# Weight rows of the first down-projection pass sent for during the last weight pair

## The chip, the cores and the metric

The kernel runs on one core of a Trainium2 chip. The metric is the device time of one execution in microseconds (us), taken as the median of the runs; lower is better. The profile and the trace come from one further execution, recorded by the hardware profiler.

The engines are PE (matrix products; PEld is its weight load), DVE (VectorE), ACT (ScalarE), POOL (GpSimd) and SP, which here only sends for transfers. POOL sends for some transfers too.

## The reference

A decoder layer: a mixing sub-layer of three branches, then a feed-forward network with a causal convolution. The change touches the second alone:

```python
h = rms_norm(x, norm_ffn_pre[l])
u = causal_dwconv(h @ w_ffn_up[l], conv_w[l], conv_b[l])
u_gate, u_val = jnp.split(u, 2, axis=-1)
f = (jax.nn.gelu(u_gate, approximate=True) * u_val) @ w_ffn_down[l]
x = x + rms_norm(f, norm_ffn_post[l])
```

There are 1024 tokens, a model width of 1024 and a hidden width of 2816, which is 22 blocks of 128 channels. Everything is float32.

## The kernel before

A product of two float32 matrices is made of three matmuls. Each operand is split into a rounded high part, made by a cast on ACT, and a low part, the difference, made by a subtraction on DVE or POOL. Function `mm3` (lines 168 to 170) issues high by high, high by low and low by high. Activations and results lie with channels in the 128 partitions and tokens along the row.

**The up-projection** runs over pairs of weight blocks, one gate block and one value block for each of the 22 hidden blocks. Pairs 5 to 21 go through `up_pairs`: each forms its 2 by 2 block product by seven products instead of eight (a Strassen scheme), each of four `mm3`. `Pair.load` sends for the weights of a pair (tiles a11, a21, a22, a12), two transfers of 128 KB for each tile, by SP into places of the pool `wp`. The places come in two classes, `self.c = i % 2`: even pairs use `whi0`, `wlo0` and `wraw0`, odd pairs `whi1`, `wlo1` and `wraw1`, with four, four and three places each (the pairs use two of the three `wraw` places at a time). Pair 21 is the last, of class 1, so that the places of class 0 are not used again once pair 20's weights have been split. `sum0` to `sum6` take the seven products out of PSUM, and `sum6` multiplies gate and value and stores the hidden block in the DRAM array `d_f`. `sum4` of the last pair calls `down_loads`, which sends for the first three rows of the down-projection.

**The down-projection** is a second such scheme, over halves of tokens, of output channels and of hidden blocks. It is seven passes (`down_pass`), each over 11 steps. A step takes an activation row f (128 hidden channels by 512 tokens, 256 KB) and a weight row u (the same 128 hidden channels by 512 output channels, 256 KB), splits both, and issues 12 matmuls into four PSUM banks named psd. Splitting is done by `step` (casts at line 1405, subtractions at line 1409): there are four places for the split u and four for the split f, so a cast for step n waits until PE has done step n - 4. The sources differ by pass:

- Pass 1: activations X, loaded from `d_f` by `f_rows` (line 1352); weights by `w_raw` (line 1363), tile name fw, 128 partitions by four runs of 512 B, into the tag `st`, which has three places. Row k + 3 can be sent for once both halves of row k's split have been made.
- Pass 2: activations R, the second half of the hidden blocks; weights Q, the sum of two blocks of the weight matrix. `Q.load` (SP) brings the first in pieces of 1 MB, 1 MB and three of 256 KB, and `Q.add` (POOL) lets an accumulating transfer add the second to it (line 1345 for both). Pieces of Q are sent for during pass 1.
- Pass 3: activations R minus another set of rows, fraw, for which there are four places; weights again by `w_raw`, into the same three places as in pass 1.

X, R and fraw rows come from `d_f`, which the pairs have written; the fraw places are those of the pairs' split weights.

**What sets the order.** Each engine works through its own queue in a fixed order, and a transfer whose place or source is not ready holds up all that SP or POOL would send after it. The order of the queues comes from a scheduler that places instructions when their operands and places are expected to be ready. `later(i, x)` tells it to put i behind x in the order, without a wait on the chip. In pass 1 both rows of step k are tied in this way to the last matmul of step k - 3.

Of the kernel before, what the change touches and what calls it, by code (L numbers as in the profile page):

```python
# [9 lines left out]
F32 = mybir.dt.float32  # L10
# [7 lines left out]
P = 128  # L18
# [10 lines left out]
NF = 22  # L29
HK = NF // 2  # L30
# [14 lines left out]
def trunk_kernel(ctx: ExitStack, tc: tile.TileContext, xT, memT, pvec, w_in, w_kv, w_upd, w_upg,  # L45
                 w_pool, w_ppool, w_pmem, w_prwkv, w_o, w_fup, w_fdn, out):
    nc = tc.nc
    V, A, G, PE, SP = nc.vector, nc.scalar, nc.gpsimd, nc.tensor, nc.sync

    const = ctx.enter_context(tc.tile_pool(name="const", bufs=1))  # L50
    wp = ctx.enter_context(tc.tile_pool(name="wp", bufs=1))
# [92 lines left out]
    def load_w(ap, nk, kp=2, c=None):  # L144
        if c is None:
            cls[0] ^= 1
            c = cls[0]
        ps = Ws()
        ps.c = c
        for k0 in range(0, nk, kp):  # L150
            load_more(ps, ap, k0, min(kp, nk - k0), kp)
        return ps
# [12 lines left out]
    def mm3(ps, w, x, start, stop):  # L165
        wh, wl = w
        xh, xl = x
        first = PE.matmul(ps, wh, xh, start=start, stop=False)  # L168
        PE.matmul(ps, wh, xl, start=False, stop=False)  # L169
        last_mm[0] = PE.matmul(ps, wl, xh, start=False, stop=stop).ins  # L170
        return first
# [36 lines left out]
    def later(i, ins, plain=False):  # L208

        tc.add_manual_dep(i if plain else i.ins, ins.name, nosync, reason="order")  # L210
# [13 lines left out]
    for k in range(KC):  # L224
        tag = ("X01", "X11", "HV", "HV")[k // 2]
# [802 lines left out]
    class Pair:  # L1028
# [46 lines left out]
            getattr(self, f"sum{n}")(ps)  # L1075

        def sum0(self, ps):
            z = [ow1.tile([P, T], F32, name=f"z{e}", tag=f"q{4 + 2 * e + self.c}") for e in range(2)]
            self.z = z
            self.c11, self.c12, self.c21, self.c22 = z[0][:, :512], z[0][:, 512:], z[1][:, :512], z[1][:, 512:]  # L1080
            self.u2 = ow.tile([P, 512], F32, name="u2", tag="xt", bufs=2)
            A.copy(self.c11, ps)
# [11 lines left out]
        def sum4(self, ps):  # L1094
            self.p7 = ps
            third = V.tensor_tensor(self.c21, self.u2, ps, op=ALU.add).ins
            if self.i == NF - 1:
                down.extend(down_loads())
                down.append(third)

        def sum5(self, ps):
# [154 lines left out]
    ahead = [load_w(w_fup[3], KC), load_w(w_fup[NF + 3], KC)]  # L1256
# [4 lines left out]
    for n in range(4):  # L1261
        j = (3, NF + 3, 4, NF + 4)[n]
# [59 lines left out]
    def panel_slots(name, tag, n0):  # L1322
        t = hf.tile([P, KC, 512], F32, name=name, tag=tag)
        return [t[:, k] for k in range(KC)] + tail_slots(name, n0)
# [26 lines left out]
    def f_rows(dst, k, n, behind=None):  # L1351
        i = SP.dma_start(dst, d_f[k][:, n * 512:n * 512 + 512])  # L1352
        if behind is not None:
            later(i, behind)
        return dst
# [5 lines left out]
    def w_raw(k, e, h, behind=None):  # L1361
        t = wp.tile([P, 512], F32, name="fw", tag="st", bufs=3).rearrange("p (j c) -> p j c", c=P)
        i = SP.dma_start(t, w_fdn[4 * e:4 * e + 4, :, HK * h + k].rearrange("j p c -> p j c"))
        if behind is not None:
            later(i, behind)
        return t

    def down_loads():

        X = panel_slots("X", "h2h0", 0)  # L1370
        return X, [(f_rows(X[k], k, 0), w_raw(k, 0, 0)) for k in range(3)]
# [22 lines left out]
    def step(x, w, places=None, behind=None):  # L1394

        n = nstep[0]
        if places is None:
            nstep[0] += 1
            f = at.tile([P, 2, 512], FR, name="f", tag=f"m{4 + n % 4}")
            u = at.tile([P, 2, 4, P], FR, name="u", tag=f"m{n % 4}")  # L1400
            u, f = ([t[:, e] for e in range(2)] for t in (u, f))
        else:
            u, f = [x.rearrange("p (j c) -> p j c", c=P) for x in places[:2]], places[2:]
        for t, src in ((u, w), (f, x)):
            hi = A.copy(t[0], src)  # L1405
            if behind is not None:
                later(hi, behind)
            on_pool = n == 1 or t is u and 3 < npass[0] < 7 and n % 2
            low = (G if on_pool else V).tensor_tensor(t[1], src, t[0].bitcast(F32), op=ALU.subtract)  # L1409
            if n < 8:  # L1410
                later(low, third if n == 0 else last_low[0] if n == 1 else last_sum[0])
        return [(u[0][:, a], u[1][:, a]) for a in range(4)], f

    log = []

    def down_pass(x, w, n, evac, side={}, post=None):
        pool, tag = ((psc, "c"), (psk, "k"))[npass[0] % 2]
        npass[0] += 1
        banks = [p_.tile([P, 512], F32, name="psd", tag=t_)
                 for p_, t_ in ((pool, tag), (psg, "g0"), (psg, "g1"), (pss, "s"))]  # L1420
        for k in range(n):
            if k in side:
                side[k]()

            if left and (n < HK or k % 2):
                for i in left.pop(0)():
                    later(i, last_mm[0])
            ws, f = step(x(k), w(k), behind=log[-3] if len(log) > 2 else None)
            if post:
                later(post(k), last_mm[0])  # L1430
            for a in range(4):
                mm3(banks[a], ws[a], f, k == 0, k == n - 1)
            log.append(last_mm[0])
        left.extend(partial(evac, a, banks[a]) for a in range(4))
# [14 lines left out]
    X, ahead, third = down  # L1449
# [6 lines left out]
    def x0(k):  # L1456
        return ahead[k][0] if k < 3 else f_rows(X[k], k, 0, log[k - 3])

    down_pass(x0, lambda k: ahead[k][1] if k < 3 else w_raw(k, 0, 0, log[k - 3]), HK, evac1,
              {3: lambda: Q.load(1, 0, 0), 5: lambda: Q.add(1, 1, 0), 7: lambda: Q.load(1, 0, 1),  # L1460
               9: lambda: Q.add(1, 1, 1)})

# [70 lines left out]
    down_pass(lambda k: X[k], lambda k: Q[k], LAST, lambda a, ps: plus(c12[a], ps), side)  # L1533
    SP.dma_start(xt, d_x1[:, :, 768:].rearrange("k p t -> p k t"))
    rest = [step(X[LAST + k], Q[LAST + k], places[k], log[k + 2 - LAST]) for k in range(HK - LAST)]
    out0(2)
    for u in left:
# [108 lines left out]
def build(arrays):  # L1646
    import numpy as np
    import concourse.bacc as bacc

    nc = bacc.Bacc("TRN2", target_bir_lowering=False, num_devices=1)  # L1650
    aps = {n: nc.dram_tensor(f"in_{n}", a.shape, mybir.dt.from_np(a.dtype), kind="ExternalInput").ap()
           for n, a in arrays.items()}
    out = nc.dram_tensor("out_T", (D, T), F32, kind="ExternalOutput").ap()
    with tile.TileContext(nc) as tc:
        trunk_kernel(tc, **aps, out=out)
    return nc
# [10 lines left out]
```

## Time and profile before

| | |
|---|---|
| median of 3 runs | 2056.73 us (2052.93 to 2056.75) |
| the profiled execution's own time | 2058.67 us |
| its span, first to last instruction | 2056.8 us |
| mean granted TensorE clock | 0.995 of full speed |
| share of busy time | PE 97%, PEld 76%, DVE 67%, ACT 52%, POOL 39% |
| SP's transfers (queue q1) | 204.44 MB, 30.7% of the 16 DMA engines' span |
| POOL's transfers (queue q0) | 14.16 MB, 4.2% |
| last matmul of the pairs, first of the down-projection | 1823.67 us, 1823.90 us |
| first and last psd matmul | 1823.90 us, 2030.69 us |

Times in the rows count from the first instruction of the span. A row of the timeline has the start, the duration, the engine, the line, the operation, the output and inputs by name, the shape and the count, and in brackets how long the engine had stood idle and what ended that. SPq is SP's queue of transfers: its rows show the sending, not the transfer. A row of transfers has the count, the size of one, and the time from sending to landing in us. In a table of stretches each engine has its busy time and, in brackets, its instructions; then come the granted clock (1.00 is full speed), the mean busy share of the 16 DMA engines, and GB/s.

### The profile page before, as it was taken

The numbers are of one execution on the slowest core, as the hardware profiler recorded it, in microseconds if no ns is written. First come the engines' busy times: TensorE is split into PE (matmuls) and PEld (weight loads), VectorE is DVE, ScalarE is ACT, GpSimd is POOL, SyncE is SP. The second block draws the span as 40 slices with busy tenths as digits, with TensorE's granted clock in tenths as the row PEclk, the third lists the DMA queues.
The fourth block names the chain that finished last, engine by engine and source line by source line (L and its number), as shares of the span: only waits on it lengthen the run. The fifth ranks groups of instructions, "written<-read, shape, count | busy, mean of one in ns | idle before, by whom it ended". The sixth has DMA issues, their size and how long they took to land. (4 is left out here: it accounts for less than half of the span.)

```text
span 2056.8 us, 34070 instructions
## 1 busy us (share of the span) xinstructions
PE 2000.2 (97%) x12246; PEld 1558.2 (76%) x12246; DVE 1378.4 (67%) x2204; ACT 1073.6 (52%) x2249; POOL 804.4 (39%) x883
## 2 busy tenths in 40 slices
PE   8999999999999999999999999999999999999997
PEld 5777767786778667776778887877678888877886
DVE  6567537663568357734596552768889888867798
ACT  7575338723773358434567343545544554444544
POOL 4521213121222121111122355655579888832441
PEclk9999999999999999999999999999999999999999
DMA  4412112120212121212525543645332222169776
GB/s 152 136 42 75 66 36 86 58 93 22 88 62 83 36 90 40 90 63 89 193 92 189 157 136 106 191 129 164 97 95 87 85 80 82 67 198 260 166 183 150
DMA packets 176714, 221.84 MB, mean 108 GB/s; under 512 B 16544, under 2 KB 128288, under 8 KB 176544
## 3 DMA queue, kind: packets, MB, share of 16 engines
q1 hardware_dynamic: 163616, 204.44, 30.7%
q0 software_dynamic: 11856, 14.16, 4.2%
q8 instruction: 97, 1.59, 0.3%
q10 hardware_dynamic: 1072, 1.05, 0.2%
q14 instruction: 73, 0.60, 0.1%
HBM read 170.30 MB, written 49.28 MB: 107 GB/s over the span
## 5 line engine op out<-in xcount | busy, mean ns | idle before, releaser
L132 POOL TENSOR_TENSOR wlo<-wraw,whi 128x256 fp32r<-128x256 f32 x472 | 412.7, 884 | 940.7 <-ACT whi L129 774.5
L168 PE MATMUL psg<-hh,whi 128*128 128x512 f32 x928 | 380.1, 410 | 2.6 <-DVE kv L315 2.6
L170 PE MATMUL psg<-hh,wlo 128*128 128x512 f32 x928 | 376.3, 406 | 0.4
L169 PE MATMUL psg<-hl,whi 128*128 128x512 f32 x928 | 375.5, 405 | 0.0
L129 ACT CAST whi<-wraw 128x256 fp32r<-128x256 f32 x472 | 182.5, 403 | 227.6 <-PE psg L169 105.7
L168 PEld LDWEIGHTS psg<-hh,whi 128*128 128x128 f32 x928 | 174.6, 188 | 43.1 <-DVE kv L315 3.8
L170 PEld LDWEIGHTS psg<-hh,wlo 128*128 128x128 f32 x928 | 174.2, 188 | 43.2 <-POOL wlo L132 5.9
L169 PEld LDWEIGHTS psg<-hl,whi 128*128 128x128 f32 x928 | 174.6, 188 | 39.4 <-issue 3.6
L1011 POOL TENSOR_TENSOR wt<-a,wt 128x256 fp32r<-128x256 f32 x136 | 156.7, 1176 | 35.6 <-ACT wt L1010 35.6
L168 PE MATMUL psd<-f,u 128*128 128x512 f32 x292 | 114.7, 393 | 3.1 <-ACT u L1405 2.4
L169 PE MATMUL psd<-f,u 128*128 128x512 f32 x292 | 114.6, 393 | 0.6 <-DVE f L1409 0.6
L170 PE MATMUL psd<-f,u 128*128 128x512 f32 x292 | 114.1, 392 | 0.0
L170 PE MATMUL psf<-h2h,wt 128*128 128x512 f32 x272 | 105.9, 389 | 1.0 <-POOL wt L1011 1.0
L169 PE MATMUL psf<-h2l,wt 128*128 128x512 f32 x272 | 105.8, 389 | 0.0
L168 PE MATMUL psf<-h2h,wt 128*128 128x512 f32 x272 | 105.8, 389 | 0.0
L1025 DVE SCALAR_TENSOR_TENSOR d<-z,pv,d 128x1023 f32<-128x1023 f32 x68 | 101.1, 1491 | 2.2
L1011 POOL TENSOR_TENSOR wt<-s,wt 128x256 fp32r<-128x256 f32 x68 | 80.3, 1201 | 3.4 <-ACT wt L1010 2.1
L686 DVE TENSOR_TENSOR HV<-ph,Hd 64x128 f32<-64x128 f32 x112 | 32.4, 289 | 72.2 <-PE ph L640 48.1
L168 PE MATMUL psf<-t,wt 128*128 128x512 f32 x204 | 79.4, 389 | 0.0
L169 PE MATMUL psf<-t,wt 128*128 128x512 f32 x204 | 79.4, 389 | 0.0
L170 PE MATMUL psf<-t,wt 128*128 128x512 f32 x204 | 79.4, 389 | 0.0
L1023 ACT ACTIVATE d<-z,pv 128x1024 f32<-128x1024 f32 x34 | 42.4, 1246 | 67.6 <-DVE z L1102 51.9
(425 smaller groups left out, 4747.0 us busy)
## 6 DMA issues: line engine op xcount, KB each, us to landing
wraw<-in_w_in SPq DMA_DIRECT2D x240, 128.0 KB, 2.4
a<-in_w_fup SPq DMA_DIRECT2D x128, 128.0 KB, 2.4
d_zg<-st SPq DMA_DIRECT2D x48, 256.0 KB, 2.7
wraw<-in_w_fup SPq DMA_DIRECT2D x80, 128.0 KB, 2.5
fw<-in_w_fdn SPq DMA_DIRECT2D x33, 256.0 KB, 4.3
fraw<-d_f SPq DMA_DIRECT2D x33, 256.0 KB, 4.5
wraw<-in_w_prwkv SPq DMA_DIRECT2D x64, 128.0 KB, 2.4
wraw<-in_w_o SPq DMA_DIRECT2D x64, 128.0 KB, 2.5
```

Of the source, the lines that this page charges most:

```text
L129: last_whi[0] = A.copy(hi, src).ins
L132: (V if lo_on_dve[0] else G).tensor_tensor(lo, src, hi.bitcast(F32), op=ALU.subtract)
L168: first = PE.matmul(ps, wh, xh, start=start, stop=False)
L169: PE.matmul(ps, wh, xl, start=False, stop=False)
L170: last_mm[0] = PE.matmul(ps, wl, xh, start=False, stop=stop).ins
L686: ready = V.tensor_tensor(HV[q, :, c + 1, e], ph[q], Hd[q], op=ALU.add).ins
L1011: low = eng.tensor_tensor(w[1][:, us], src[u], w[0][:, us].bitcast(F32), op=ALU.subtract)
L1023: A.activation(d, z, AF.Identity, scale=col("cw2", j), bias=col("cb", j))
L1025: V.scalar_tensor_tensor(d[:, n:], z[:, :T - n], col(cw, j), d[:, n:], op0=ALU.mult, op1=ALU.add)
```

## The change

Eight of the eleven weight rows of pass 1, rows 3 to 10, no longer go through `w_raw`. A new function `w_early` sends for each as two transfers of 128 KB (two of the four runs of 512 B each), tile name fe, into places of the pairs' weights: rows 3 to 7 from `sum0` of pair 21 into class 0 (places of pair 20: four `whi0`, four `wlo0`, two `wraw0`), rows 8 to 10 from `sum4` of pair 21 into class 1 (four `whi1`, two `wlo1`). Rows 0 to 2 are loaded as before. `step` splits a row that comes in two tiles by two casts and two subtractions of 128 x 256.

```diff
         def sum0(self, ps):
+            if self.i == NF - 1:
+                w_early(1 - self.c, range(3, 8))
             z = [ow1.tile([P, T], F32, name=f"z{e}", tag=f"q{4 + 2 * e + self.c}") for e in range(2)]
...
             if self.i == NF - 1:
                 down.extend(down_loads())
+                w_early(self.c, range(8, HK))
                 down.append(third)
...
+    w_first = {}
+
+    def w_early(c, ks):
+        tags = [(f"whi{c}", 4)] * 4 + [(f"wlo{c}", 4)] * 4 + [(f"wraw{c}", 3)] * 2
+        for k in ks:
+            w_first[k] = []
+            for u in range(2):
+                tag, bufs = tags.pop(0)
+                t = wp.tile([P, 2, P], F32, name="fe", tag=tag, bufs=bufs)
+                SP.dma_start(t, w_fdn[2 * u:2 * u + 2, :, k].rearrange("j p c -> p j c"))
+                w_first[k].append(t)
...
-        for t, src in ((u, w), (f, x)):
+        split_u = [([p[:, 2 * m:2 * m + 2] for p in u], w[m]) for m in range(2)] if isinstance(w, list) else [(u, w)]
+        for t, src in (*split_u, (f, x)):
             hi = A.copy(t[0], src)
...
-    down_pass(x0, lambda k: ahead[k][1] if k < 3 else w_raw(k, 0, 0, log[k - 3]), HK, evac1,
+    down_pass(x0, lambda k: ahead[k][1] if k < 3 else w_first[k], HK, evac1,
```

On SP, before, from the first three X rows (a fence shows rows in the order in which the engine works through them, with line, operation, output and input, and a count of equal neighbours):

```order
L1352 DMA X<-d_f 128x512 x3
L1352 DMA fraw<-d_f 128x512 x3
L1352 DMA X<-d_f 128x512
L1363 DMA fw<-in_w_fdn 128x4x128
L1352 DMA X<-d_f 128x512
L1363 DMA fw<-in_w_fdn 128x4x128
L1345 DMA Q<-in_w_fdn 128x4x512
L1352 DMA X<-d_f 128x512
L1363 DMA fw<-in_w_fdn 128x4x128
L1352 DMA X<-d_f 128x512
L1363 DMA fw<-in_w_fdn 128x4x128
L1352 DMA X<-d_f 128x512
```

After this, three more X rows follow, each behind a weight row, and then the first R rows. With the change the same place reads, from the store of pair 20's block (d_f<-d; its lines are 3 higher here):

```order
L1116 DMA d_f<-d_18123 128x1024
L1366 DMA fw<-in_w_fdn 128x4x128
L1355 DMA X<-d_f 128x512 x3
L1355 DMA fraw<-d_f 128x512
L1366 DMA fw<-in_w_fdn 128x4x128
L1355 DMA fraw<-d_f 128x512
L1366 DMA fw<-in_w_fdn 128x4x128
L1355 DMA fraw<-d_f 128x512
L1355 DMA X<-d_f 128x512 x2
L1348 DMA Q<-in_w_fdn 128x4x512
L1355 DMA X<-d_f 128x512 x4
L1348 DMA Q<-in_w_fdn 128x4x512
```

The three fw rows here are the first three of pass 3, whose places are now free sooner; two X rows and four R rows follow the last row shown. No weight row of pass 1 is left between the X rows. The fe transfers stand ahead of this piece: one among pair 21's own weights, nine between the stores of pairs 18 and 19, and six between that of pair 19 and the first fraw row:

```order
L1116 DMA d_f<-d_17761 128x1024
L1380 DMA fe<-in_w_fdn 128x2x128 x9
L1116 DMA d_f<-d_17942 128x1024
L1380 DMA fe<-in_w_fdn 128x2x128 x6
L1355 DMA fraw<-d_f 128x512
```

Before, nothing stood between those two stores, nor between the second and the fraw row. The other place is ACT in the later half of pass 1, the casts of steps 7 to 11 (u<-Q is the first weight row of pass 2, step 11; f<-R its activation row). Before:

```order
L1405 CAST u<-fw 128x512
L1405 CAST u<-Q 128x512
L1405 CAST f<-X 128x512
L1405 CAST u<-fw 128x512
L1405 CAST f<-X 128x512
L1405 CAST u<-fw 128x512
L1405 CAST f<-R 128x512
```

The first row here is the weight row of step 8. With the change, from the two halves of the weight row of step 8:

```order
L1421 CAST u<-fe 128x256 x2
L1421 CAST f<-X 128x512
L1421 CAST u<-fe 128x256 x4
L1421 CAST u<-Q 128x512
L1421 CAST f<-X 128x512 x2
L1421 CAST f<-R 128x512
```

The weight rows of steps 9, 10 and 11 now all stand ahead of the activation rows of steps 9 and 10. The subtractions on DVE stand in the same order as these casts.

## The prediction

> **What bounds the kernel now.** I read the share of TensorE first, then busy time by stretch, then the starts of the matmuls, and last who released the late ones. PE is busy for 97% of the span, so at most some tens of microseconds can be won anywhere, and only where PE stands still. The stretches around the end of the last weight pair (1785 to 1824) and the down-projection passes, each row giving length, busy time and count by engine, the granted clock, the DMA engines' share and GB/s:
>
> ```profile
> core 0: us, PE busy (x) PEld busy (x) DVE busy (x) ACT busy (x) POOL busy (x), PEclk, DMA share, GB/s
> 1785.00:1815.00 30.00, 30.00 (x134) 24.86 (x133) 26.06 (x28) 16.20 (x33) 24.64 (x20) 1.00 0.12 45
> 1815.00:1824.00 9.00, 9.00 (x41) 7.44 (x41) 5.81 (x9) 3.10 (x4) 1.29 (x2) 1.00 0.45 146
> 1824.00:1845.00 21.00, 21.00 (x95) 17.38 (x94) 14.01 (x18) 10.38 (x14) 2.11 (x2) 1.00 0.97 281
> 1845.00:1855.00 10.00, 7.62 (x26) 5.58 (x25) 4.47 (x7) 4.70 (x9) 1.28 (x1) 0.83 1.09 346
> 1855.00:1882.00 27.00, 27.00 (x120) 22.32 (x119) 22.78 (x36) 11.14 (x21) 7.72 (x6) 1.00 1.16 276
> 1882.00:1900.00 18.00, 16.83 (x69) 12.49 (x68) 10.29 (x17) 7.20 (x14) 2.54 (x2) 1.00 1.15 237
> ```
>
> DMA is nearly idle (0.12) while the last two pairs run, and from 1824 to 1900 it is full (0.97 to 1.16). PE issues 95 matmuls in the 21 us from 1824, but 26 in the 10 us from 1845, some at a clock of 0.83, and 69 in the 18 us from 1882. How late that makes it, the first matmuls of passes 1, 2 and 4 show, with the two long waits between:
>
> ```profile
> 1823.90 0.39 PE L168 MATMUL psd<-f,u 128*128 128x512 f32 x1
> ...
> 1845.43 0.39 PE L170 MATMUL psd<-f,u 128*128 128x512 f32 x1
> 1848.20 0.50 PE L168 MATMUL psd<-f,u 128*128 128x512 f32 x1 [2.38 <-ACT u L1405]
> ...
> 1858.21 0.39 PE L168 MATMUL psd<-f,u 128*128 128x512 f32 x1
> ...
> 1887.10 0.50 PE L168 MATMUL psd<-f,u 128*128 128x512 f32 x1 [0.65 <-ACT f L1405]
> ...
> 1920.73 0.39 PE L168 MATMUL psd<-f,u 128*128 128x512 f32 x1
> ```
>
> Undisturbed, a matmul follows every 0.2267 us (from 1823.90, 95 of them later, 1845.43), so a step of 12 takes 2.72 us and a pass of 11 steps 29.92. Pass 2 ought to start at 1853.82 and starts at 1858.21: **4.39 us lost in pass 1**. Pass 4 ought to start at 1913.66 and starts at 1920.73: 7.07 in all, so **2.68 more in passes 2 and 3**. Of the 4.39, the pause before step 8 (counting from 0) is 2.54, and the rest, 1.85, is the slow clock behind it. Who is waited for, on ACT, which casts each weight row (u) and each activation row (f) in one fixed order:
>
> ```profile
> 1847.53 0.62 ACT L1405 CAST u<-fw 128x512 fp32r<-128x512 f32 x1 [4.99 <-DMA fw<-in_w_fdn]
> 1848.06 0.61 ACT L1405 CAST u<-Q 128x512 fp32r<-128x512 f32 x1
> 1850.85 0.62 ACT L1405 CAST f<-X 128x512 fp32r<-128x512 f32 x1 [2.17 <-DMA X<-d_f]
> ...
> 1886.43 0.62 ACT L1405 CAST f<-R 128x512 fp32r<-128x512 f32 x1 [3.02 <-DMA R<-d_f]
> ```
>
> The first stall is a weight row (step 8), then an activation row (step 9); the second is the last activation row of pass 2. When these were sent for, on SP, and how long single ones took to land:
>
> ```profile
> 1818.69 5.76 SPq L1352 DMA_DIRECT2D fraw<-d_f  x3
> 1824.50 0.42 SPq L1352 DMA_DIRECT2D X<-d_f  x1
> ...
> 1826.47 0.50 SPq L1345 DMA_DIRECT2D Q<-in_w_fdn  x1
> ...
> 1836.85 0.37 SPq L1363 DMA_DIRECT2D fw<-in_w_fdn  x1
> ...
> 1838.00 0.68 SPq L1352 DMA_DIRECT2D X<-d_f  x1
> ...
> 1840.59 3.78 SPq L1352 DMA_DIRECT2D X<-d_f  x1
> ...
> 1861.69 1.60 SPq L1352 DMA_DIRECT2D R<-d_f  x2
> ...
> 1875.58 0.40 SPq L1352 DMA_DIRECT2D R<-d_f  x1
> ```
>
> ```profile
> fw<-in_w_fdn SPq DMA_DIRECT2D x1, 256.0 KB, 10.6
> ...
> Q<-in_w_fdn POOLq DMA_DIRECT2D x1, 1024.0 KB, 12.7
> ...
> R<-d_f SPq DMA_DIRECT2D x1, 256.0 KB, 10.8
> ```
>
> The row of step 8 goes out at 1836.85 and lands 10.6 us later. It goes out so late because its place is one of three that turn over, and the X rows stand behind such weight rows on SP.
>
> **The change part by part.** *Removed from 1824 to 1855:* eight rows of 256 KB, 2.1 MB. At the 281 GB/s of the row 1824 to 1845 that is 7.5 us of a full DMA. *Added before 1815:* 16 transfers of 128 KB where the share is 0.12. Their price on SP, and that of the split casts:
>
> ```profile
> 1762.61 13.75 SPq L1040 DMA_DIRECT2D a<-in_w_fup  x8
> 1776.46 17.89 SPq L1113 DMA_DIRECT2D d_f<-d  x2
> ```
>
> ```profile
> a<-in_w_fup SPq DMA_DIRECT2D x128, 128.0 KB, 2.4
> ```
>
> ```profile
> L1405 ACT CAST u<-fw 128x512 fp32r<-128x512 f32 x16 | 9.8, 621 | 15.4 <-DMA fw<-in_w_fdn 15.3
> ...
> L1010 ACT CAST wt<-a 128x256 fp32r<-128x256 f32 x14 | 5.3, 403 | 4.9 <-issue 2.2 <-POOL wt L1011 2.0 <-DVE a L1018 0.5
> ```
>
> Every pair before sends for its eight transfers within such 13.75 us and a transfer lands in 2.4. The first ten new ones follow that pattern one pair later (84 matmuls, 19.04 us on, 1781.7 to 1795.4), so the second store of the row above, pair 19's, goes out at about 1795.5 instead of 1794.0, as those of the pairs before it did. The last six wait for places that pair 21 frees, and end near 1809 by the same count of products, ahead of the first X rows. I cost this stretch at nothing; PE's full busy time there is the cover, and if a store or a fraw came 2 us later, nothing on PE waits for it before 1853. Casting a row in two pieces costs ACT 2 x 0.403 - 0.621 = 0.19 us; VectorE's subtraction is bounded by nothing and by as much again as the 0.69 of the whole one. Eight rows: 1.5 us of ACT and up to 5.5 of DVE, beside 10.6 and 7.0 us in which they stood idle from 1824 to 1845. I take nothing.
>
> *Moved:* with their places free earlier, three rows of pass 3 now go out before 1824 (before the change, between 1845 and 1855), another 0.8 MB out of the full stretch; and no X row waits behind a weight row on SP. X rows 3 and 4 stay behind the fraw rows (until 1824.50), but X8, X9 and X10 go out at about 1827.5, 1828.5 and 1829, the last two instead of 1838.00 and 1840.59. Ahead of X8 lie one fraw, five X and the first Q load, 2.6 MB or 9 us at 281 GB/s: landed by about 1835, against a need at 1844. X10 has another 1.5 MB ahead, 5.4 us, and lands by about 1842, or 1846 if the accumulating load below takes half of the engines meanwhile; it is needed at about 1849.5.
>
> *What becomes late next:* ACT's order, before and now, has the cast of pass 2's first weight row (u<-Q) ahead of the cast of X9. At 1848.06 it waited for nothing, since the late fw row stood before it; now it is the last to come. It needs this piece of Q whole, loaded and then added to by an accumulating load of POOL. This load's course before, and the packets and engine shares of POOL's queue (q0) and SP's (q1), first from 1840 to 1844, then from 1876 to 1888:
>
> ```profile
> 1831.73 0.78 POOL L1113 DMA_DIRECT2D d_f<-d  x1 [9.71 <-DVE d L1112]
> 1834.49 1.33 POOL L1345 DMA_DIRECT2D Q<-in_w_fdn  x1 [1.97 <-DMA Q<-in_w_fdn]
> ```
>
> ```profile
> q0 software_dynamic: 338, 0.69, 93.2%
> q1 hardware_dynamic: 278, 0.16, 18.7%
> ```
>
> ```profile
> q0 software_dynamic: 830, 1.61, 72.7%
> q1 hardware_dynamic: 799, 1.46, 37.6%
> ```
>
> It landed at 1834.49 + 12.7 = 1847.2. Now it can start 1 to 2 us earlier, since the Q load has two weight rows fewer ahead, but not before POOL's store at 1831.73 has been issued. In the first window one of its packets took 0.932 x 4 x 16 / 338 = 0.176 us and one of SP's 0.043; in the second 0.168 and 0.090. The two queues moved about packet for packet. With rows of X, Q and R beside it instead of the small packets of fw, 512 packets take 512 x 0.26 / 16 = 8.3 us instead of 7.0. So I let it land at 1846.6, between 1845 and 1848.5. Step 9 is due at 1823.90 + 9 x 2.72 = 1848.38; u<-Q and the X9 cast take 0.53 + 0.62 (starts 1847.53 and 1848.06, and a cast's length), so PE waits only if the landing is later than 1847.2. Cost: 0.3 us, from nothing to 1.3.
>
> *The second stall:* pass 2's R rows (the fifth and sixth at 1861.69, the last at 1875.58) went out late because SP stood behind weight rows and behind fraw rows whose places wait for DVE. Without weight rows, the fifth goes out near 1852, when DVE has freed the first fraw place, and each later one behind a subtraction that frees a fraw place, one per step of 2.72 us: the last near 1867. A landing of 10.8 us, as before, brings it at 1878; due is step 10 of pass 2, 1823.90 + 21 x 2.72 = 1881.0, less 1.3 for cast and subtraction. I take 2.3 of the 2.68 as gained, between nothing and all.
>
> *Sum:* 4.39 - 0.3 + 2.3 = **6.4 us**. The profiled execution took 2058.67 us (span 2056.8 and 1.9 around it); it would take 2052.3. The median of the three runs, 2056.73, lies 1.9 below it, so the forecast is **2050.3**. The later passes only move forward, since their loads wait for places, not for the clock.
>
> [...]
>
> **The rivals.** *One stall stays* (25%). Passes 2 and 3 stay as late as they were, since DMA was full there too (1.15) and the accumulating loads are untouched: 4.1 gained, 2052.6. Or step 9 waits 1 to 3 us and the slow clock follows. Times from 2051.3 to 2054.7. Against it: 2.9 MB, some 10 us of DMA, leave the stretch, and its lost time was 7.07.
>
> *The stall only changes its name* (15%). The weight rows were one of two that were late: X9 held ACT at 1850.85 as well. If DMA stays as full, X and Q rows take their place, and the time is 2056.7 within 2. For it: once fw had come, the cast of X9 waited another 2.17 us of its own. Against it: SP now sends X9 nearly 10 us earlier.
>
> *Slower* (8%). One mechanism: the first accumulating load, now beside denser traffic of SP's, lands so late that u<-Q blocks the X9 cast behind it in ACT's order. A later 1 MB load of the same kind took 18.1 us:
>
> ```profile
> Q<-in_w_fdn POOLq DMA_DIRECT2D x1, 1024.0 KB, 18.1
> ```
>
> From 1834.49 that is 1852.6, and step 9 would start at 1853.8, 5.4 late, with 1.85 for the clock and the 2.68 of the second stall untouched: 9.9 against 7.07, so 2059.6. It decides from 15.2 us on, where the three sum to 7.07. Against it: that load stood behind others on POOL's queue, this one behind a store alone. [...]
>
> **How the numbers follow.** Forecast case (both stalls nearly gone, 5.4 to 7.5 gained, 2049.2 to 2051.3): 52%. Range 2048.6 to 2056.5: it reaches through the second case and into the third, and leaves out the slower end and a little above the full gain. A measurement can tell about 0.2%, 4.1 us, from no change: faster than 2052.6 are the first case and under half of the second, 63%; within it 30%; slower 7%.
>
> **What would show it.** Right: no pause before step 8, no clock under 1.00 from 1845 to 1855, pass 2 starting 29.9 to 30.3 us after pass 1, and the wait of f for R gone near pass 2's end. Wrong: a wait of ACT's u for Q longer than 1 us ahead of step 9; f still waiting for R; or a pause of PE before the first down-projection step, which would put the cost into the pairs.

## The result, and the profile after

| | before | after |
|---|---|---|
| median | 2056.47 us (2052.93 to 2059.88, 15 runs) | 2051.00 us (2047.86 to 2055.44, 15 runs) |
| ratio, with its 95% interval | | 0.9976 [0.9969, 0.9984] |
| the profiled execution's own time, and its span | 2058.67, 2056.8 us | 2050.06, 2048.4 us |

The change makes the kernel 5.5 us faster by the medians, and the ratio lies 0.24% below 1, its interval clear of 1. (Two executions in the sets below are so far off that the ratios leave them out: one of bytes_back, 3226 us at a mean clock of 0.554, and one of before, 5926 us.) The page of the changed kernel gives TensorE the same share as before:

```profile
span 2048.4 us, 34107 instructions
...
PE 1996.5 (97%) x12246; PEld 1558.6 (76%) x12246; DVE 1378.9 (67%) x2212; ACT 1073.7 (52%) x2257; POOL 802.9 (39%) x883
```

The stretches of the prediction, in the changed kernel:

```profile
core 0: us, PE busy (x) PEld busy (x) DVE busy (x) ACT busy (x) POOL busy (x), PEclk, DMA share, GB/s
1785.00:1815.00 30.00, 30.00 (x134) 24.84 (x133) 24.55 (x25) 14.59 (x28) 22.76 (x18) 1.00 0.32 104
1815.00:1824.00 9.00, 9.00 (x41) 7.45 (x40) 7.33 (x10) 4.50 (x6) 1.29 (x1) 1.00 0.76 218
1824.00:1845.00 21.00, 21.00 (x95) 17.38 (x94) 13.31 (x26) 10.73 (x24) 3.38 (x3) 1.00 1.05 316
1845.00:1855.00 10.00, 8.94 (x40) 7.06 (x39) 8.49 (x14) 6.00 (x11) 1.25 (x2) 1.00 1.03 249
1855.00:1882.00 27.00, 27.00 (x121) 22.36 (x120) 23.10 (x36) 13.37 (x24) 9.00 (x8) 1.00 1.14 259
1882.00:1900.00 18.00, 18.00 (x81) 14.92 (x80) 12.37 (x21) 9.23 (x17) 0.00 (x0) 1.00 0.77 172
```

The transfers have moved into the stretch in which DMA was nearly idle (0.12 before, 0.32 now), and PE's busy time there is whole, as it was. From 1845 to 1855 PE issues 40 matmuls instead of 26, and the clock stays at 1.00 where it was 0.83. From 1882 to 1900 PE is full. The DMA engines are as busy as before until 1882: the room that the weight rows left was filled by rows that now start earlier.

The first matmuls of passes 1, 2, 3 and 4, and the one long wait between:

```profile
1821.14 0.39 PE L168 MATMUL psd<-f,u 128*128 128x512 f32 x1
...
1846.84 1.20 PE L168 MATMUL psd<-f,u 128*128 128x512 f32 x4 [1.06 <-ACT f L1421]
...
1852.44 0.39 PE L168 MATMUL psd<-f,u 128*128 128x512 f32 x1
...
1882.36 0.39 PE L168 MATMUL psd<-f,u 128*128 128x512 f32 x1
...
1912.28 0.39 PE L168 MATMUL psd<-f,u 128*128 128x512 f32 x1
```

Pass 2 starts 31.30 us after pass 1, 1.38 more than the 29.92 of an undisturbed pass (1.37 with the pitch unrounded), and passes 2 and 3 take 29.92 each. So 1.37 us are lost where it was 4.39, and nothing where it was 2.68: **5.70 us won**, 3.02 in pass 1 and 2.68 behind it. The medians say 5.5.

The two spans differ by 8.4 us, 2.7 more than that. This part lies ahead of the change: the first psd matmul starts 2.76 earlier. A row of the profile of before, and then one of after, shows where much of it arose, at the program's start, where PE ran at a clock of 0.79 in one execution and of 1.00 in the other:

```profile
40.00:48.00 8.00, 6.28 (x11) 2.78 (x12) 7.81 (x14) 6.80 (x12) 0.00 (x0) 0.79 0.01 2
```

```profile
40.00:48.00 8.00, 7.33 (x23) 4.45 (x24) 8.00 (x14) 7.54 (x12) 1.39 (x2) 1.00 0.00 1
```

One pair of spans would overstate this change by half. Therefore every kernel below is read in two ways: by its times, and by the time that it loses between the first psd matmul and the start of pass 4 (three undisturbed passes are 89.76 us).

### The profile page after: what moved, and what is told of

Its sections match the earlier page's. It is cut to its first block, busy times and chain, and to the rows that moved or that the text cites. A ratio compares the mean times of both kernels' runs of the same rounds, so it can differ in the third digit from the quotient of the medians.

```text
span 2048.4 us, 34107 instructions
## 1 busy us (share of the span) xinstructions
PE 1996.5 (97%) x12246; PEld 1558.6 (76%) x12246; DVE 1378.9 (67%) x2212; ACT 1073.7 (52%) x2257; POOL 802.9 (39%) x883
## 4 chain that ended last, share of the span: by engine, by line
PE 38%; DVE 5%; DMA 4%; issue 2%; POOL 2%; ACT 1%; SPq 0%; ACTq 0%; POOLq 0%; DVEq 0%
PE psf L170 5%; PE psf L169 5%; PE psf L168 5%; PE psg L168 4%; PE psg L169 4%; PE psg L170 4%; PE psd L169 3%; PE psd L170 3%; PE psd L168 3%; DMA g<-d_zg 2%; POOL wlo L132 1%; DMA Q<-in_w_fdn 1%; DVE o L1213 1%; DVE h2l L123 1%; DMA wraw<-in_w_fup 0%
## 5 line engine op out<-in xcount | busy, mean ns | idle before, releaser
L168 PEld LDWEIGHTS psg<-hh,whi 128*128 128x128 f32 x928 | 174.5, 188 | 43.1 <-DVE kv L315 3.9
```

## The experiments

Three questions were open: what is behind the 1.37 us that stay; whether the first stall went because of the bytes, the order of sending or the split rows; and why the second stall went. Each run was measured beside the kernel before on the same chip, and its ratio is to the runs of before in its own set, whose medians were 2056.47, 2057.41, 2056.86 and 2056.97. So compare ratios rather than medians.

| kernel | median (runs) | ratio [95%] | lost in pass 1 | in passes 2 and 3 | last R sent, after pass 2's start |
|---|---|---|---|---|---|
| before | 2056.47 (15) | 1 | 4.39 | 2.68 | 17.37 |
| after | 2051.00 (15) | 0.9976 [0.9969, 0.9984] | 1.37 | 0.00 | 13.46 |
| cast_order | 2049.66 (5) | 0.9965 [0.9952, 0.9979] | 0.00 | 0.00 | 13.14 |
| cast_order_again | 2048.85 (7) | 0.9960 [0.9946, 0.9975] | 0.00 | 0.00 | 13.74 |
| order_xfirst | 2051.10 (9) | 0.9974 [0.9965, 0.9984] | 0.00 | 0.00 | 12.74 |
| store_sp | 2059.85 (1) | | 8.56 | 0.00 | 11.44 |
| bytes_back | 2057.12 (10) | 0.9995 [0.9986, 1.0004] | 5.35 | 0.25 | 14.06 |
| x_first | 2055.46 (10) | 0.9988 [0.9977, 0.9999] | 2.57 | 2.20 | 16.88 |
| halves_only | 2057.96 (10) | 1.0002 [0.9993, 1.0011] | 4.04 | 4.20 | 18.30 |
| rows_3_7 | 2053.03 (10) | 0.9987 [0.9975, 0.9999] | 5.13 | 0.15 | 13.98 |
| rows_8_10 | 2056.68 (10) | 1.0000 [0.9991, 1.0009] | 5.55 | 0.00 | 13.55 |
| fw_rows_late | 2047.93 (7) | 0.9963 [0.9951, 0.9974] | 0.00 | 0.33 | 14.91 |
| r_one_late | 2050.03 (1) | | 0.00 | 3.98 | 20.55 |
| r_two_late | 2061.82 (10) | 1.0024 [1.0015, 1.0034] | 0.00 | 11.83 | 27.60 |

The last three columns are worked out from the starts of the matmuls of one profiled execution each, and the send row of the last R.

### The rest of 1.37 us: cast_order, order_xfirst, store_sp

In the changed kernel ACT stands still ahead of step 9, not for its own rows, but for the weight row of step 11:

```profile
1845.65 0.62 ACT L1421 CAST u<-Q 128x512 fp32r<-128x512 f32 x1 [4.55 <-DMA Q<-in_w_fdn]
1846.18 1.13 ACT L1421 CAST f<-X 128x512 fp32r<-128x512 f32 x2
```

Behind the wait of 4.55 us two casts of X rows follow with no wait: X9 and X10 had landed. PE's wait of 1.06 ends with the first of them. In cast_order this cast is put behind the two:

```diff
         for t, src in (*split_u, (f, x)):
             hi = A.copy(t[0], src)
+            if places is None and t is f:
+                last_f[0] = hi.ins
+            elif n == HK and places is None:
+                later(hi, last_f[0])
```

> The changed kernel, with the cast of pass 2's first weight row (u<-Q) tied behind the casts of X9 and X10 on ACT. Main theory: the 1.37 us that PE still loses before step 9 come from u<-Q waiting for the accumulating load with the X9 cast behind it. Then the pause goes, pass 2 starts 29.9 to 30.1 us after pass 1 (31.29 in the changed kernel), and the time falls by 1.2 to 1.4 us against it, some 5.5 to 7.5 us against the kernel before. Rival: X9 itself lands late, at about the same time as Q, because the accumulating load takes two thirds of the DMA engines. Then the X9 cast shows a wait on its own transfer, PE's pause stays within 0.3 us of 1.37, and the time is that of the changed kernel.

```profile
1842.93 0.62 ACT L1422 CAST f<-X 128x512 fp32r<-128x512 f32 x1 [1.48 <-DMA X<-d_f]
...
1845.24 0.62 ACT L1422 CAST u<-Q 128x512 fp32r<-128x512 f32 x1 [1.69 <-DMA Q<-in_w_fdn]
```

The rows of ACT in cast_order show the X cast ahead. Its own wait of 1.48 and the wait for Q, both still there, now cost nothing: PE runs from the first psd matmul into pass 4 without a pause. The 1.37 us were an order of two casts. Repeated beside three others on another occasion it gave 2048.85:

> The kernel of cast_order once more, beside the three others on one chip, for its time. Waiting of the X casts behind u<-Q was all that was left: 1.4 us under the changed kernel, 2049.6, ratio 0.9969. If the cast order were worth nothing: 2051.0, ratio 0.9976. The two differ by less than the interval, so the trace decides: 0.0 us late at the start of pass 4 against 1.4.

The intervals of after and of cast_order overlap; that it is faster by some 1.4 us rests on the trace, and the medians of both runs lie on that side.

store_sp goes the other way. In the changed kernel, pair 21's store is sent by SP instead of POOL; on SP it stands ahead of the first Q load, which so goes out at 1831.61, 7.8 us after the first psd matmul, where it was 1.5.

```diff
-            (G if self.i == NF - 1 else SP).dma_start(d_f[self.i], d1)
+            SP.dma_start(d_f[self.i], d1)
```

> The changed kernel with the store of pair 21's block sent by SP instead of POOL, where the order puts it ahead of the first Q load, so that SP stands until DVE has made the block, some 6 us, and Q and X5 to X10 go out that much later. Main theory (u<-Q holds the X9 cast, and the accumulating load takes some 8.5 us beside SP's rows): the load lands 3 to 5 us later against the start of pass 1, and PE's pause before step 9 grows from 1.37 to between 5 and 9 us with the slow clock, more than all that the change won. Rival (without the store ahead of it on POOL's queue the load starts at once and gains back what the Q load lost): the pause stays under 2.5 us.

POOL's, ACT's and PE's rows of store_sp:

```profile
1838.33 1.45 POOL L1348 DMA_DIRECT2D Q<-in_w_fdn  x1 [15.58 <-DMA Q<-in_w_fdn]
```

```profile
1853.22 0.62 ACT L1421 CAST u<-Q 128x512 fp32r<-128x512 f32 x1 [7.61 <-DMA Q<-in_w_fdn]
```

```profile
1854.41 2.07 PE L168 MATMUL psd<-f,u 128*128 128x512 f32 x4 [4.12 <-ACT f L1421]
```

The accumulating load starts 4.5 us later after the first psd matmul than in the changed kernel (14.5 against 10.0), PE's wait at step 9 is 4.12 instead of 1.06, and pass 1 loses 8.56. This is one half of the prediction's slower rival: a late landing lets u<-Q block the X9 cast, and in the changed kernel that stayed small. The other half, a load slowed to some 18 us by denser traffic, did not come about: the load took 14.8 us here and 14.4 in the changed kernel, and was late because it started late. That the time of its one run, 2059.85, is near the 2059.6 worked out for the rival is chance, since that sum holds a second stall and this run has none. Six X rows now stand behind the store too and cost part of the 8.56 (1.85 are lost ahead of step 8); the run doesn't separate them.

order_xfirst adds to cast_order the sending of all X rows as early as SP reaches them (`f_rows(X[k], k, 0)` without `log[k - 3]`).

> The kernel of cast_order (the changed kernel with u<-Q behind the casts of X9 and X10), and the X rows besides no longer tied to pass 1's matmuls, so that all eleven go out before the fraw rows. Main theory: no time is left to win in the passes, since PE was late by 0.00 us at pass 4 in cast_order; the time stays within 1.5 us of it, 2048 to 2051, and only the DMA share before 1824 rises. Rival: the earlier X rows let Q be complete sooner and pull in the passes behind it, 1 to 2 us faster than cast_order.

Nothing was late any more in cast_order, and nothing is won: 0.9974, an interval that overlaps with cast_order's.

### What ended the first stall: bytes_back, x_first, halves_only, rows_3_7, rows_8_10

bytes_back leaves the change as it is and sends, beside each of X3 to X10, 256 KB of the same weight rows into a tile that nothing reads: these 2.1 MB are in the full stretch again, while PE's operands come from the early rows.

```diff
+    dm = hf.tile([P, KC, 512], F32, name="dm", tag="h2l1")
+
     def x0(k):
-        return ahead[k][0] if k < 3 else f_rows(X[k], k, 0, log[k - 3])
+        if k < 3:
+            return ahead[k][0]
+        x = f_rows(X[k], k, 0, log[k - 3])
+        later(SP.dma_start(dm[:, k - 3].rearrange("p (j c) -> p j c", c=P),
+                           w_fdn[0:4, :, k].rearrange("j p c -> p j c")), log[k - 3])
+        return x
```

> The changed kernel, and beside it eight loads of 256 KB of the same weight rows in the place where they were sent for before (behind X3 to X10 on SP), into a place that nothing reads. Main theory (the DMA engines were full, and the 2.1 MB are what was won): they are full again, so half or more of the 5.7 us comes back as waits of ACT for X, Q and R; 3 to 6 us slower than the changed kernel, between 2053 and 2057. Rival (the order on SP and the three turning places were what was late, not the bytes): these loads wait for no place, X goes out as early as without them but for 0.4 us of sending each, and the time stays within 1.5 us of the changed kernel.

SP's and ACT's rows of bytes_back; the X row of 1836.22 is X10:

```profile
1832.49 2.02 SPq L1355 DMA_DIRECT2D X<-d_f  x1
...
1836.22 5.04 SPq L1355 DMA_DIRECT2D X<-d_f  x1
```

```profile
1844.10 0.62 ACT L1421 CAST u<-Q 128x512 fp32r<-128x512 f32 x1 [3.94 <-DMA Q<-in_w_fdn]
...
1847.58 0.62 ACT L1421 CAST f<-X 128x512 fp32r<-128x512 f32 x1 [2.86 <-DMA X<-d_f]
...
1849.20 0.62 ACT L1421 CAST f<-X 128x512 fp32r<-128x512 f32 x1 [1.00 <-DMA X<-d_f]
```

Single sends of SP stretch to 5.04 us although none of the added loads waits for a place, and X10 goes out 16.0 us after the first psd matmul, where it was 6.5 in the changed kernel and 16.7 before the change. X9 and X10 hold up ACT by 2.86 and 1.00, and pass 1 loses 5.35 us, more than before the change. Q is no later than in the changed kernel: u<-Q starts 23.9 us after that matmul against 24.5. The time is that of before (0.9995). So it isn't enough that the weight rows are there in good time: what they take away from the X rows has to go too. This is the prediction's rival "The stall only changes its name", brought about, with X rows alone in the weight rows' place. The expected rival, that X would go out as early as without these loads, failed.

x_first is the kernel before, with no weight row moved and only the X rows sent as early as SP reaches them:

```diff
-        return ahead[k][0] if k < 3 else f_rows(X[k], k, 0, log[k - 3])
+        return ahead[k][0] if k < 3 else f_rows(X[k], k, 0)
```

> The kernel before, with the X rows no longer tied to the matmuls of pass 1: all eleven go out in one piece as soon as their places are free, before the fraw rows (about 1816 to 1821); the weight rows stay where they were, in three turning places. Main theory: the weight rows of steps 8 to 10 still wait for places and for a full DMA, but 1.5 MB of X move into the stretch that was half empty, so a part of the gain comes without moving any weight row: 2 to 5 us faster than the kernel before, with ACT still waiting for fw. Rival (weight rows alone are what was late): the first stall stays at 4 to 4.5 us and the time within 1 us of the kernel before. Second rival (the order of X behind fw was all of it): the whole 5.7 us are gained.

```profile
1846.97 0.62 ACT L1405 CAST u<-fw 128x512 fp32r<-128x512 f32 x1 [6.58 <-DMA fw<-in_w_fdn]
```

ACT has run ahead and so stands idle longer, but the weight row of step 8 comes sooner than before: its cast starts 22.7 us after the first psd matmul instead of 23.6. No X row is waited for any more. Pass 1 loses 2.57 instead of 4.39: 1.2 at step 3, where PE waits for DVE's subtraction of a weight row, 0.4 ahead of step 8 and 0.9 ahead of step 9. Sending X early alone brings 0.12% [0.01%, 0.23%], and 2.3 of 7.07 us in the trace, the low end of what was expected; the rest needs the weight rows moved as well.

halves_only splits rows 3 to 10 in halves in the kernel before, as the changed `step` does, and changes nothing else.

```diff
+        halves = places is None and 3 <= n < HK
+        split_u = [([p[:, 2 * m:2 * m + 2] for p in u], w[:, 2 * m:2 * m + 2]) for m in range(2)] if halves else [(u, w)]
-        for t, src in ((u, w), (f, x)):
+        for t, src in (*split_u, (f, x)):
```

> The kernel before, with the weight rows 3 to 10 of pass 1 split by two casts and two subtractions of 128 x 256 each, and loaded as before. It measures the price of the smaller pieces alone. Main theory: hidden, within 0.5 us of the kernel before, ACT 1.5 us busier. Rival: each row's split comes later by 0.3 to 0.5 us, its place in the three turning ones comes free later, and the first stall grows by 0.5 to 3 us.

The time is unchanged, 1.0002. (Its one profiled execution lost 8.24, 1.2 more than that of before, all of it in passes 2 and 3; ten runs don't show it.) Two of its rows matter for the price of a slow clock, taken up at the end.

rows_3_7 and rows_8_10 move only five, or only three, of the eight rows; the others go through `w_raw` as before.

```diff
-                w_early(self.c, range(8, HK))
...
-    down_pass(x0, lambda k: ahead[k][1] if k < 3 else w_first[k], HK, evac1,
+    down_pass(x0, lambda k: ahead[k][1] if k < 3 else w_first[k] if k in w_first else w_raw(k, 0, 0, log[k - 3]), HK, evac1,
```

(This is rows_3_7; rows_8_10 takes the call in `sum0` away instead.)

> The changed kernel with rows 3 to 7 alone sent for early; rows 8 to 10 go through the three turning places again. Main theory (bytes out of the full stretch): 1.3 of the 2.1 MB leave it, and rows 8 to 10 find their places free at once, since rows 0 to 2 are long done: PE late by 1.4 to 3 us at pass 4, time 1 us above the changed kernel at most 2.5. Rival (the late rows are those of steps 8 to 10, and only they count): the first stall stays at 3 us or more and the time within 2 us of the kernel before.

> The changed kernel with rows 8 to 10 alone sent for early; rows 3 to 7 go through the three turning places as before. Main theory (bytes): 0.8 MB leave the full stretch, a third of the gain, PE late by 3 to 5.5 us at pass 4, 1.5 to 4 us faster than the kernel before. Rival (the late rows alone count): steps 8 to 10 never wait for a weight row, the first stall is gone but for 1.4 us as in the changed kernel, and 4 to 6 us are gained.

ACT's longest waits, first in rows_3_7, then in rows_8_10:

```profile
1846.77 0.62 ACT L1420 CAST u<-Q 128x512 fp32r<-128x512 f32 x1 [8.43 <-DMA Q<-in_w_fdn]
...
1853.59 0.62 ACT L1420 CAST u<-fw 128x512 fp32r<-128x512 f32 x1 [4.64 <-DMA fw<-in_w_fdn]
```

```profile
1846.88 0.62 ACT L1419 CAST f<-X 128x512 fp32r<-128x512 f32 x1 [6.45 <-DMA X<-d_f]
```

With five rows moved, the weight row of step 10 is late: it is sent for at 1833.21, takes 20.4 us to land, and PE waits 2.73 us for it. The long wait for Q costs only 0.6 us. With three rows moved, the X rows behind the other five are late, and PE waits 3.12 us ahead of step 8. In the traces neither part alone helps pass 1 (5.13 and 5.55 lost), and both together leave 1.37: the parts don't add. The times agree for rows_8_10 (1.0000), where both expectations failed. Those of rows_3_7 spread from 2050.30 to 2059.72; their ratio, 0.9987, is worth some 2.7 us, within what was expected, while the profiled execution, one of the slower ones (2056.43), won 1.8 and lost more than was expected, so what moving these five rows is worth stays open. Both kernels end the second stall, which alone is worth 0.1%, too little for these times to tell.

### What ended the second stall: fw_rows_late, r_one_late, r_two_late

In the table no kernel whose last R row goes out within 14.1 us of pass 2's start loses more than 0.25 us in passes 2 and 3, and all in which it goes out at 16.9 or later lose 2.2 or more. Three edits of cast_order, which loses nothing, were made to see whether this is a cause. fw_rows_late sends the first three weight rows of pass 3 behind the first R rows, as before the change (0.8 MB back in the full stretch):

```diff
-    down_pass(t3, lambda k: w_raw(k, 1, 0), HK, evac7,
+    down_pass(t3, lambda k: w_raw(k, 1, 0, log[8 + k] if k < 3 else None), HK, evac7,
```

> The casts in the new order as in cast_order, and beside it the first three weight rows of pass 3 tied to steps 8 to 10 of pass 1, so that they go out behind the first R rows, in the full stretch, as they did before the change: 0.8 MB back in it. Their places are long free, so that SP waits for none of them. Theory of the sending time: SP isn't held up, the fifth R row goes out within 1 us of pass 2's start, and under 0.5 us are lost by the start of pass 4; time near 2050. Rival, the bytes: the full stretch carries 0.8 MB more, 2.5 to 3 us of full DMA, and 1 to 3 us are lost near the end of pass 2; time 2051 to 2053.

It lost nothing in pass 2 and 0.33 in pass 3, and is as fast as cast_order: these bytes aren't it. (bytes_back put the other 2.1 MB back, and lost nothing in pass 2 either; no run put back both.) r_two_late moves no byte; it ties R4 to R10 of pass 2 two steps later, so that SP sends each behind two more fraw rows, and r_one_late does so by one step:

```diff
-    down_pass(lambda k: f_rows(R[k], HK + k, 1, log[HK + k - 5]), lambda k: Q[k], HK, evac3,
+    down_pass(lambda k: f_rows(R[k], HK + k, 1, log[HK + k - (5 if k < 4 else 3)]), lambda k: Q[k], HK, evac3,
```

> The casts in the new order as in cast_order, and beside it the activation rows R 4 to 10 of pass 2 tied to matmuls two steps later, so that SP sends each behind two more fraw rows. No byte more or less. In cast_order the fifth R went out 1.0 us before pass 2 started and the last 13.1 us after it, and no time was lost. Theory of the sending time: the second stall comes when the R rows go out late against pass 2's start (2.2 to 4.2 us lost in the kernels where the last one went 16.9 to 18.3 us after it, under 0.3 where it went 13.1 to 14.1 after). Two steps later is about 18.5 us after: ACT's f waits for the last R rows, PE pauses near the end of pass 2, and 2 to 4 us are lost by the start of pass 4; time 2052 to 2054. Rival, the bytes: the stall came from the 2.9 MB that stood in the full stretch; nothing is added here, so under 0.5 us lost and the time of cast_order, 2050.

> As r_two_late with one step instead of two: the last R goes out about 15.8 us after pass 2's start, between the kernels without a loss (13.1 to 14.1) and those with one (16.9 to 18.3). By the sending time between 0 and 2 us lost; by the bytes none.

SP's rows of r_two_late at its last R row, with DVE's row that frees the fraw place, and then ACT's and PE's rows of the step before (step 9):

```profile
1879.07 0.69 DVE L1458 TENSOR_TENSOR R<-R,fraw 128x512 f32<-128x512 f32 x1
```

```profile
1879.79 0.32 SPq L1355 DMA_DIRECT2D fraw<-d_f  x1
1880.20 0.43 SPq L1355 DMA_DIRECT2D R<-d_f  x1
```

```profile
1885.13 0.62 ACT L1422 CAST f<-R 128x512 fp32r<-128x512 f32 x1 [5.30 <-DMA R<-d_f]
```

```profile
1885.80 0.79 PE L168 MATMUL psd<-f,u 128*128 128x512 f32 x1 [3.88 <-ACT f L1422]
```

The stall returns, and grows with the delay: 0.00, 3.98, 11.83 us lost for none, one and two steps, and for two steps 2061.82 against 2048.85 in the time. (The one run of r_one_late took 2050.03; its first psd matmul came 4 us sooner than that of cast_order_again, so this time says nothing of the 3.98.) Sending the R rows later is thus enough to bring such a stall about, with no byte more; that it is also what made the stall before the change rests on the table, where before, x_first and halves_only send the last R row 16.9 us or more after pass 2's start and lose 2.2 or more, and no other kernel, r_one_late and r_two_late apart, loses over 0.33. The sizes were wrong in my expectations (0 to 2 us for one step, 2 to 4 for two), and the last row went out later than counted (15.8 and 18.5 us after pass 2's start). The reason as the rows suggest it: an R row that lands late holds up ACT's f cast, DVE's subtractions behind it (f, then R less fraw), and so the freeing of the next fraw place, behind which SP sends the next R row. The rows above show one such turn: the subtraction ends at 1879.76, the fraw row goes out at 1879.79 and R behind it. The delay goes round this loop. One and two steps are 2.7 and 5.4 us; the last row went out 20.55 and 27.60 us after pass 2's start instead of 13.74. Of the 11.83, some 5 us build up while the clock is at half behind two of the pauses (0.50 in both windows, 10.2 us in all); over its whole span r_one_late had a mean clock of 0.998, r_two_late 0.993.

What had delayed these rows before the change? SP's row of the three small Q loads, which stand directly ahead of the fifth and sixth R row, before the change and then after it:

```profile
1856.41 5.24 SPq L1345 DMA_DIRECT2D Q<-in_w_fdn  x3
```

```profile
1849.92 1.53 SPq L1348 DMA_DIRECT2D Q<-in_w_fdn  x3
1851.50 0.98 SPq L1355 DMA_DIRECT2D R<-d_f  x2
...
1865.90 0.39 SPq L1355 DMA_DIRECT2D R<-d_f  x1
```

Sending three rows took 5.24 us instead of 1.53. Meanwhile, the load of the queues, before (from 1856.3 to 1861.8) and after (from 1849.8 to 1851.6):

```profile
q0 software_dynamic: 322, 0.63, 61.5%
q1 hardware_dynamic: 1158, 0.82, 49.5%
```

```profile
q1 hardware_dynamic: 149, 0.25, 47.6%
q0 software_dynamic: 58, 0.09, 28.3%
```

Before, SP sent into engines whose busy shares for the two queues add up to 111%, half of that for an accumulating load; after, they add up to 76%. The fifth R row went out 3.48 us after pass 2's start before the change, and 0.94 ahead of it after: 4.42 apart, of which the sending of Q is 3.71. That full engines slow the sending is read from these rows and those of bytes_back; no run varied it alone.

## Why the prediction was right, and where its sizes were off

- **Where the time was lost, and that the change frees it:** right. Pass 1's pause before step 8 is gone, the clock is 1.00 there, and of 7.07 us 5.70 are won, where 6.4 were forecast. One of its two sizes was misread, though: the prediction put 1.85 of the 4.39 down to the slow clock. The weight row of step 9 was late as well:

```profile
1851.71 0.62 ACT L1405 CAST u<-fw 128x512 fp32r<-128x512 f32 x1 [0.25 <-DMA fw<-in_w_fdn]
```

A matmul starts 0.67 us behind such a cast (1847.53 and 1848.20), so at full clock step 9 would have begun near 1852.4 instead of 1852.74. By this estimate the slow clock cost some 0.4 us, and the late rows the rest. halves_only agrees: it lost 4.04 in pass 1 with the clock at 1.00 there. The sum used the 4.39 whole and is untouched; the price in the slower rival is not.
- **The fe loads cost nothing:** right. SP's rows show the last one sent by 1805.7 (forecast 1809), the last six landed in 2.2 us each, with PE full beside them, and pair 19's store out at 1793.02 (forecast 1795.5). This execution runs 2.8 us ahead of the one that the forecasts count in:

```profile
1779.12 13.81 SPq L1380 DMA_DIRECT2D fe<-in_w_fdn  x8
1793.02 0.42 SPq L1116 DMA_DIRECT2D d_f<-d  x1
...
1798.16 7.49 SPq L1380 DMA_DIRECT2D fe<-in_w_fdn  x6
```

```profile
fe<-in_w_fdn SPq DMA_DIRECT2D x6, 128.0 KB, 2.2
```

- **The split casts cost nothing:** right as far as can be told. halves_only's time is within 0.1% of before, and cast_order, with the same split rows, loses nothing up to pass 4.
- **"Cost: 0.3 us, from nothing to 1.3" at step 9:** the mechanism is right, as cast_order shows, and this is the term that was mis-sized: 1.37, just outside its own bounds. Two signs that the prediction had named for itself speak against it here: u waited for Q over 1 us (4.55), and pass 2 started 31.30 us after pass 1 instead of 29.9 to 30.3. The accumulating load, as POOL's row and the row of its landing show it:

```profile
1831.14 1.33 POOL L1348 DMA_DIRECT2D Q<-in_w_fdn  x1 [1.54 <-DMA Q<-in_w_fdn]
```

```profile
Q<-in_w_fdn POOLq DMA_DIRECT2D x1, 1024.0 KB, 14.4
```

It landed 24.4 us after the first psd matmul (1831.14 + 14.4 - 1821.14); forecast were 22.7, and at most 24.6. Most of this is its start, 10.0 us after that matmul, only 0.6 earlier than before, where 1 to 2 had been counted; it waited for the plain Q load still. Its length was nearly right (14.0 forecast): from 1836 to 1846 the two queues moved 656 and 703 packets.

```profile
q0 software_dynamic: 656, 1.31, 70.6%
q1 hardware_dynamic: 703, 1.28, 39.2%
```

That is about packet for packet, 656 against 703, as the prediction had it, at 0.172 and 0.089 us each (0.706 x 10 x 16 / 656, and the same of q1).
- **The second stall, "2.3 of the 2.68":** right in sign and place, all 2.68 were won. Counted from the first psd matmul, the fifth R row went out at 30.4 us (forecast 28.1), the last at 44.8 (43.1), and its cast, which waited for its landing, began at 56.6 (landing forecast 54.1): 1.7 to 2.5 later than forecast, 1.4 of it the lateness of pass 1. The need was at about 57.2, as step 10 began at 1879.64 and the splitting takes 1.3. The step's reason was partly wrong: it was not weight rows that SP stood behind just then, but the sending of three Q rows into full engines. And the margin is small, 0.6 us. The sign "f still waiting for R" was there too, with 3.18 us on ACT, but PE did not feel it: a wait on ACT alone was a poor sign.
- **The rivals:** none came about whole in the changed kernel. Half of "One stall stays" did: step 9 waited within its 1 to 3 us (1.37), but no slow clock followed, the second stall went all the same, and the time, 2051.0, is in the forecast case. "The stall only changes its name" was brought about on the chip by bytes_back, and the late accumulating load of "Slower" by store_sp, there by a late start.

Sum as measured: 4.39 - 1.37 + 2.68 = 5.70; forecast 4.39 - 0.3 + 2.3 = 6.4. The medians, 2051.0 against a forecast of 2050.3, differ by the same 0.7 us. That the two agree to the tenth is luck: the interval of the ratio is 3 us wide, and the forecast started from a median of three runs, 2056.73, which fifteen runs put at 2056.47.

## What to carry to other kernels

Where a full stretch of DMA follows an idle one (here shares of 0.97 to 1.16 from 1824 to 1900 us, 0.12 until 1815; 5.70 us won), move what can be sent early, and then look at what each engine now waits for in its own order: a cast for a later step that waits for the last transfer holds up those for the next step (here 1.37 us, won back by an order of two casts in cast_order, with fw_rows_late the fastest kind of kernel here). Where transfers, casts and places feed each other in a ring, a delay of one step need not cost one step: here R rows tied 2.7 and 5.4 us later cost 3.98 and 11.83 (the latter with 10.2 us at a clock of 0.50). And time lost should be counted at the place of the change, by the starts of PE's work, since spans of single executions differ by more than such a change is worth (here by 8.4 us for 5.70).

## What the hardware showed unexpectedly

A pause of PE of about 2 us was followed by 3.4 us at half the clock in some executions and not in others. The pause of 2.38 us of before stands in the prediction; PE's rows of r_two_late and then of halves_only show two more:

```profile
1871.02 0.53 PE L168 MATMUL psd<-f,u 128*128 128x512 f32 x1 [1.95 <-ACT f L1422]
```

```profile
1846.43 0.50 PE L168 MATMUL psd<-f,u 128*128 128x512 f32 x1 [2.27 <-ACT u L1407]
```

The windows behind the three, in the order before, r_two_late, halves_only (the clock is the third number from the end):

```profile
1848.60:1852.00 3.40, 3.40 (x9) 2.48 (x8) 1.38 (x3) 0.98 (x3) 1.28 (x1) 0.50 1.11 340
```

```profile
1871.40:1874.80 3.40, 3.21 (x8) 2.47 (x8) 2.86 (x6) 1.71 (x4) 1.48 (x2) 0.50 0.69 217
```

```profile
1846.40:1850.00 3.60, 3.04 (x12) 2.11 (x12) 1.50 (x4) 1.43 (x3) 1.16 (x1) 1.00 1.11 347
```

So the length of the pause alone doesn't decide here: 1.95 and 2.38 us were followed by half clock, 2.27 was not. The traces of before and after show where such stretches begin. Ahead of its last psd matmul, before has four, each 3.41 us long at a clock of 0.50, at 42.92, 1241.00, 1408.25 and 1848.57 us, which is 1198.08, 167.25 and 440.32 us apart; after has two, also at 0.50, at 1236.49 (6.83 us long) and 1407.16 (3.41), 170.67 apart. Measured in these two traces, the four distances are 351, 49, 129 and 50 times the same 3.4133 us (440.32 / 129) within 0.01. Which pause is followed by such a stretch and which is not, no run shows.

The price of such a stretch depends on what else is late. In before it was some 0.4 us, by the estimate above. A second pause of halves_only shows how a late row takes its place, at full clock (1.00 from 1850 to 1854):

```profile
1850.60 0.73 PE L168 MATMUL psd<-f,u 128*128 128x512 f32 x2 [1.13 <-ACT u L1407]
```

In r_two_late it came on top of the wait: behind its pause of 3.88 us another 3.1 us were lost over 6.8 us at half clock, although ACT cast step 10's row at 1887.48, a microsecond before step 10 was due at full speed (1885.80 + 2.72).
